# Layer 1's first shift and scale: from column-tiled matmuls in one attention stage to DVE row sums in the next

## The chip, the cores and the metric

The kernel runs on one core of a Trainium2 chip. The metric is the device time of one execution in microseconds (us). The core has five engines that work side by side, each through its own list of instructions in order: TensorE (PE, with its weight loads shown apart as PEld), VectorE (DVE), ScalarE (ACT), GpSimd (POOL) and SyncE (SP). Transfers between HBM and the core's memory (SBUF) are issued by SP or POOL and run on the DMA engines. TensorE writes to PSUM, eight banks of 512 fp32 values in each of 128 partitions.

## The reference, cut to what matters

The model has two layers over 512 latent tokens x and 256 context tokens ctx, all 1024 wide. Each layer turns the conditioning vectors (c for x, c_ctx for ctx) into six vectors of 1024 values: shift, scale and gate of the mixer, and the same three of the feed-forward part.

```
silu_c, silu_cc = silu(c), silu(c_ctx)
for layer in range(2):
    mod  = silu_c  @ w_mod[layer] + b_mod[layer]      # 6 x 1024 values, for x
    modc = silu_cc @ w_mod[layer] + b_mod[layer]      # 6 x 1024 values, for ctx
    sh1, sc1, g1, sh2, sc2, g2 = split(mod, 6)
    h  = rms_norm(x)   * (1 + sc1)  + sh1
    hc = rms_norm(ctx) * (1 + csc1) + csh1
    y, yc = mixer(h, hc)                              # layer 0: two kinds of attention
    x = x + g1 * y;   x = x + g2 * swiglu(norm(x, sc2, sh2))
    # the same two updates for ctx, in layer 0 only
```

The change concerns `sh1` and `sc1` of layer 1, for both streams: 2048 of the 6144 values of `mod` and of `modc`. These need the first 2048 columns of `w_mod[1]`, 8 MB in fp32, and are first used by the first norm of layer 1.

## The kernel before, in words

Work is feature-major: a stream is a tile of 128 partitions by 8 feature blocks by tokens. A projection multiplies in fp32 by splitting each operand in a high and a low part; `mm3` (L422 to L424) issues three matmuls for each block. `weight` (L133 to L145) loads a weight tile of 512 KB on SP's queue, rounds it on ACT (L143) and takes the rest on DVE (L145).

The program is written as Python generators. A main generator yields after each small step; `aside` keeps a list of other generators and `step(n)` advances them by n steps, so that their instructions are written between those of the main one. From this the framework's planner makes the order of each engine's list: of the instructions that are ready it takes those written first. A tile gets its memory when it is first used. A pool keeps, for each tag, a number of buffers (`bufs`); where all are in use, a new tile of this tag waits until the last access of the tile that holds one, wherever in the program this access is written. `keep_in_program_order` ties an instruction behind the one written just before it on the same engine; later ones may still pass it.

Layer 0 up to its output projection has these stages:

1. The input projection (`even_in`). The residual X (tile `xx`, 2 MB, the only buffer of its tag in pool `xz`) has been read by then. `rest()` takes that buffer anew as `xs` and `self.scratch`, and its quarters serve as `raws`, four buffers for modulation weights. `mods(0, 1)` and `mods(0, 2)` run aside (layer 0's other four vectors).
2. The first attention stage: attention of the 256 context tokens (8 head pairs), the rest of the queries, and the first 2 (`N1`) of the 8 head pairs of the latent tokens. PSUM: a=4, e=2, v=2 banks. Aside, at half a step for each step (`F0`): what is left of the queries, then `mods(1, 0)`, the subject of the change.
3. The second attention stage: the other 6 latent head pairs (`main`; 60 steps). PSUM: a=3, e=2, v=1, b=2. Aside, at 0.8 of a step for each (`F1`), `ctx_rest`: layer 0's output projection, norm and feed-forward part of the context stream, 76 weight tiles. It uses bank tag `b`, and `self.scratch` as room for squares and activations (`sq_a1`, `sq1`, `nm_t1`, `ff_a1`).
4. X is loaded again (`self.stream(0, self.ins["xt"])`, L200), and the latent stream's output projection (`onto`) follows, beside layer 1's context chain and `mod_rows(1, range(16, 48))`, which computes the other four vectors of layer 1, for x alone, as row sums on DVE.

In an attention step (`attend`, L628 to L652), PE writes the scores to `a` banks, DVE takes the maximum and adds the bias (L635, L639), ACT takes the exponential (L640, L642), PE transposes the result through two `e` banks (L650), DVE and ACT copy it out (L652), and PE multiplies it with the values (L678). At the end of a pair `normalise` uses a POOL copy (L664) and an `e` bank (L374).

`mods` holds the vector silu(c), padded to 32 columns, as the stationary operand in four column strips of the array at once and streams the weights past it (L230), 256 matmuls and 16 transfers of 512 KB on POOL's queue (L218) for one group of 2048 values; it holds one `e` bank while a quarter is accumulated, then copies (L240), transposes (L244) and adds the bias (L248). `mod_rows` spreads silu(c) along the free dimension once (transposes through `spread`, L374, and a copy, L264), and then has, for every 128 values, one transfer of 512 KB (L272) and one DVE instruction that multiplies and sums (L279).

Of the kernel before, what the change touches and what calls it, by code (L numbers as in the profile page):

```python
# [13 lines left out]
ALU = mybir.AluOpType  # L14
# [3 lines left out]
P = 128  # L18
NX, NCTX = 512, 256
NT = NX + NCTX  # L20
KD = 8
# [16 lines left out]
MI, F0, F1, O0 = 3, 0.5, 0.8, 1.4  # L38
M0, C1, B0, B1, B2, L0, L1, L2, L3 = 0.5, 1.6, 24, 2.3, 0.1, 0.5, 1.75, 1.4, 1.7

MG = 2

H0, H1, H2, H3 = 2, 2, 4, 4

# [25 lines left out]
class Net:  # L70
# [132 lines left out]
    def mods(self, l, g, tmp, raws, dma, tag="t", hold=False):  # L203
# [48 lines left out]
                yield  # L252
        yield

    def mod_rows(self, l, tiles, tmp, dma, tag):


        nc, V = self.nc, self.nc.vector
        s = self.t(tmp, [P, 1024], "silu_r", bufs=1)
        for h in range(2):  # L260
            ps = self.bank(tag)
            for j in range(4):
                self.spread(ps[:, P * j : P * j + P], self.sc[:, 4 * h + j, 0:1].broadcast_to([P, P]))
            nc.scalar.copy(s[:, 512 * h : 512 * h + 512], ps)  # L264
        V.memset(self.mod[l][:, tiles[0] : tiles[-1] + 1, 1], 0.0)
        todo, ahead = iter(tiles), []

        def load():
            t = next(todo, None)
            if t is not None:  # L270
                ahead.append(self.t(tmp, [P, 1024], "wmod", bufs=3))
                dma(ahead[-1], self.ins[f"wmodT{l}"][t - tiles[0]])  # L272

        load(), load(), load()
        yield
        for t in tiles:
            w = ahead.pop(0)
            self.tc.keep_in_program_order(
                V.tensor_tensor_reduce(w, w, s, 1.0, self.bmod[:, l, t : t + 1], ALU.mult, ALU.add, self.mod[l][:, t, 0:1])  # L279
            )  # L280
            load()
            yield
# [560 lines left out]
    def layer0(self):  # L843
        nc, V = self.nc, self.nc.vector
        with ExitStack() as c1:
# [8 lines left out]
            with ExitStack() as c2:  # L854
                ap_ = self.pool(c2, "attn0", 1)
                aq = ap_
                kst = self.t(ap_, [P, 8, NT], "kst", F32R)
                raws = [self.t(ap_, [P, 8, NX], f"qx{i}") for i in range(2)]
                vt = self.t(ap_, [P, TTILES, 256], "vt")
                cq = c2.enter_context(ExitStack())  # L860
                ap_ = self.pool(cq, "attnc", 1)
                tmp = Slots(self.t(ap_, [P, 16 * NCTX], "qc"), 2)
                start = self.start(tmp, [r[:, 4 * i : 4 * i + 4, :] for r in raws for i in range(2)], {0: hx, 1: hc})
                next(start)
                cp = self.cp
                self.cp = aq
                self.mband = self.const("mband", [P, 3 * P])
                self.sinkc = self.t(aq, [P, 8, 4], "sinkc")
                sk = self.const("sink", [P, 8])
                V.memset(self.sinkc, NEG)  # L870
                V.tensor_copy(self.sinkc[:, :, 0], sk)
                self.cp = cp
                c3 = c2.enter_context(ExitStack())
                tmp = self.pool(c3, "in0", 1)
                self.cp = tmp
                self.cos, self.sin = self.const("cos", [P, XTILES, HD]), self.const("sin", [P, XTILES, HD])
                self.cp = cp
                qx = qc = spare = None

                def rest():  # L880
                    nonlocal qx, qc, raws, spare
                    qx = [self.t(aq, [P, 8, NX], f"qx{i}", F32R) for i in range(2)]
                    qc = self.t(ap_, [P, 2, 8, NCTX], "qc", F32R)
                    qc = [qc[:, i] for i in range(2)]
                    xs = self.scratch = self.t(self.xz, [P, KD, NX], "xx")
                    cs = self.t(self.xz, [P, KD, NCTX], "xc").rearrange("p k n -> p (k n)")
                    raws = [xs[:, 2 * i : 2 * i + 2, :] for i in range(4)]
                    spare = Slots(cs, 2)
                    self.qg, self.kg = (self.t(spare, [P, HD], i, bufs=1) for i in ("qg", "kg"))
                    nc.gpsimd.dma_start(self.qg, self.ins["qg"])  # L890
                    nc.gpsimd.dma_start(self.kg, self.ins["kg"])
                    self.aside(*[self.mods(0, g, spare, raws, nc.gpsimd.dma_start) for g in (1, 2)[:MG]])
                    V.tensor_scalar(self.qg, self.qg, SCALE, None, op0=ALU.mult)
                    tabs = []
                    for g in (self.qg, self.kg):
                        C, S = self.t(tmp, [P, XTILES, HD], "gc", bufs=2), self.t(tmp, [P, XTILES, HD], "gs", bufs=2)
                        gb = g.unsqueeze(1)
                        V.tensor_tensor(C, self.cos, gb.broadcast_to([P, XTILES, HD]), op=ALU.mult)
                        for a, b in ((0, 32), (32, 0)):
                            V.tensor_tensor(  # L900
                                S[:, :, a : a + 32], self.sin[:, :, a : a + 32],
                                gb[:, :, b : b + 32].broadcast_to([P, XTILES, 32]), op=ALU.mult,
                            )
                        tabs.append((C, S))
                    (self.cq, self.sq), (self.ck, self.sk) = tabs
                    return list(zip(qx, qc))

                queries = self.even_in(tmp, hx, hc, kst, vt, start, rest)
                self.finish()
                cw.close()  # L910
                cps.close()
                with ExitStack() as cA:
                    tmp = self.pool(cA, "at0", 3, side="right")
                    xy = [(hx[0][y], hx[1][y]) for y in range(KD)]
                    cy = [(hc[0][y], hc[1][y]) for y in range(KD)]

                    def pairs(i, ys, blocks, q):
                        for br in range(2):
                            for pr in range(4):
                                yield self.even_pair(tmp, br, pr, blocks, q[br], kst, vt, ys[4 * br + pr])  # L920

                    def chain(gens):
                        for g in gens:
                            yield from g

                    main = chain(itertools.islice(pairs(0, xy, range(4), qx), N1, None))
                    with ExitStack() as c4:
                        self.psum(c4, a=4, e=2, v=2)
                        self.aside(queries, *[self.mods(*g, spare, raws, nc.gpsimd.dma_start, "e") for g in ((0, 1), (0, 2), (1, 0))[MG:]])
                        side = chain(itertools.islice(pairs(0, xy, range(4), qx), N1))  # L930
                        for i, _ in enumerate(chain(pairs(1, cy, (4, 5), qc))):
                            if i % 4 < N1:
                                next(side, None)
                            self.step(F0)
                        for _ in side:
                            self.step(F0)
                        self.finish()
                    c3.close()
                    cq.close()
                    with ExitStack() as c4:  # L940
                        self.psum(c4, a=3, e=2, v=1, b=2)
                        self.aside(self.ctx_rest(hc))
                        for _ in main:
                            self.step(F1)
                        self.finish()
            cC.close()
            self.stream(0, self.ins["xt"])
            self.layer1_open()
# [778 lines left out]
def prep(inputs):  # L1727
# [3 lines left out]
    g = {k: np.asarray(v) for k, v in inputs.items()}  # L1731
    f32 = np.float32
    c_ = np.ascontiguousarray
    d = {}
# [2 lines left out]
    cc = np.stack([g["c"][0], g["c_ctx"]], 1).reshape(KD, P, 2).transpose(1, 0, 2)  # L1737
    for l in range(2):
        for h in range(3):
            if (l, h) < (1, 1):  # L1740
                w = g["w_mod"][l][:, 2048 * h : 2048 * h + 2048].reshape(KD, P, 4, 4, P).transpose(3, 1, 0, 2, 4)
                d[f"wmod{l}{h}"] = c_(w.reshape(4, P, KD, 4 * P))
    d["wmodT1"] = c_(g["w_mod"][1][:, 2048:].T.reshape(32, P, KD * P))
    bmod = g["b_mod"].reshape(2, 48, P).transpose(2, 0, 1)
    nr = np.stack([g["norm_mix"][0], g["norm_ffn"][0], g["norm_mix"][1], g["norm_ffn"][1], g["norm_out"]])
    nr = nr.reshape(5, KD, P).transpose(2, 0, 1)
# [1 line left out]
    w = g["w_in_even"][0]  # L1748
# [3 lines left out]
    def tiles(w):  # L1752
        k, n = w.shape
        return w.reshape(k // P, P, n // P, P).transpose(2, 1, 0, 3).reshape(n // P, P, k)
# [17 lines left out]
    w = tiles(g["w_in_odd"][0])  # L1772
    d["w1in"] = c_(w)
    t = np.arange(P)
# [31 lines left out]
    i, j = np.arange(P)[:, None], np.arange(P)[None, :]  # L1806
# [21 lines left out]
```

## Time and profile before

| | us |
|---|---|
| median of 3 runs (2052.88 to 2057.1) | 2054.01 |
| the profiled execution | 2053.72 |
| its span, first to last instruction | 2051.9 |
| PE busy in the span | 1956.0 |
| DVE busy | 1261.4 |
| ACT busy | 893.7 |

The profile is of one execution. Busy time is the time in which an engine's records lie; matmul records overlap, since matmuls are pipelined, so the distance between starts tells what one costs in a row of them. A row of a group view gives line, engine, operation, tiles (out<-in), shapes and count, then the busy time in us and the mean of one in ns, then the idle time just before them and what ended it. A row of a timeline gives start, length (both us), engine, line, operation, tiles and count, and in brackets an idle time before it and its releaser. A row of the windows view gives start:end, length, then for each engine busy us and count, the granted clock of TensorE (1.00 is full), the mean share of the DMA engines and GB/s.

### The profile page before, as it was taken

How to read it: one execution, taken by the hardware profiler on the slowest of the kernel's cores; microseconds unless marked ns; L12 is line 12 of the kernel's file. 1: busy time of each engine (PE TensorE's matmuls, PEld its weight loads, DVE VectorE, ACT ScalarE, POOL GpSimd, SP SyncE). 2: the span in 40 equal slices, each digit the busy share in tenths (PEclk: the TensorE clock that was granted, in tenths of full speed). 3: DMA queues.
4: the chain of work that ended last, by engine and by line, in shares of the span. 5: the costliest groups of instructions: out<-in, count | busy, mean ns of one | idle time of the engine just before them, and what ended most of it. 6: DMA issues, size and time to landing. Idle time of an engine off the chain costs nothing.

```text
span 2051.9 us, 37913 instructions
## 1 busy us (share of the span) xinstructions
PE 1956.0 (95%) x15360; PEld 1606.6 (78%) x15360; DVE 1261.4 (61%) x2504; ACT 893.7 (44%) x1681; POOL 163.0 (8%) x326
## 2 busy tenths in 40 slices
PE   7999999999988999999999999899899989999997
PEld 6776778999987888777777777677667778888887
DVE  5656667666657554659746767787757773333335
ACT  4335556766733433553222346545345453222221
POOL 0111100000010001000112000102322000000000
PEclk9999999999999999999999999999799999999999
DMA  7453422434484345545533323455665133332321
GB/s 277 148 182 124 145 91 74 145 115 128 133 268 141 109 128 164 157 147 154 179 125 117 111 73 98 130 173 174 171 198 146 52 98 113 93 101 85 106 90 50
DMA packets 109918, 272.64 MB, mean 133 GB/s; under 512 B 14736, under 2 KB 48176, under 8 KB 106800
## 3 DMA queue, kind: packets, MB, share of 16 engines
q1 hardware_dynamic: 97520, 224.74, 35.5%
q0 software_dynamic: 12224, 45.49, 6.8%
q8 instruction: 121, 1.98, 0.4%
q14 instruction: 53, 0.43, 0.1%
HBM read 238.20 MB, written 31.98 MB: 132 GB/s over the span
## 4 chain that ended last, share of the span: by engine, by line
PE 78%; DVE 10%; issue 6%; DMA 3%; ACT 2%; POOL 0%; DVEq 0%; ACTq 0%; SPq 0%; POOLq 0%
PE ps_b L422 17%; PE ps_b L423 17%; PE ps_b L424 17%; PE ps_v L678 4%; PE ps_a L628 2%; PE ps_e L650 2%; PE ps_w L1351 2%; PE ps_w L1357 2%; DVE wlo L145 1%; PE ps_s L1380 1%; DMA xx<-in_wmod 1%; PE ps_w L1370 1%; PE ps_e L1258 1%; PE ps_w L1389 1%; DVE kb L1295 1%
## 5 line engine op out<-in xcount | busy, mean ns | idle before, releaser
L143 ACT CAST whi<-wraw 128x1024 fp32r<-128x1024 f32 (+2 forms) x291 | 292.6, 1008 | 664.1 <-PE ps_b L423 526.3
L145 DVE TENSOR_TENSOR wlo<-wraw,whi 128x1024 fp32r<-128x1024 f32 (+2 forms) x291 | 340.8, 1172 | 235.5 <-ACT whi L143 229.3
L422 PE MATMUL ps_b<-hxh,whi 128*128 128x512 f32 (+1 forms) x1040 | 402.4, 390 | 15.8 <-ACT cj L1018 6.7
L423 PE MATMUL ps_b<-hxl,whi 128*128 128x512 f32 (+1 forms) x1040 | 398.4, 385 | 2.1 <-DVE hxl L415 1.9
L424 PE MATMUL ps_b<-hxh,wlo 128*128 128x512 f32 (+1 forms) x1040 | 396.6, 383 | 2.2 <-DVE wlo L145 2.2
L422 PEld LDWEIGHTS ps_b<-hxh,whi 128*128 128x128 f32 x1040 | 199.1, 193 | 59.0 <-ACT cj L1018 7.2
L423 PEld LDWEIGHTS ps_b<-hxl,whi 128*128 128x128 f32 x1040 | 199.2, 192 | 40.7 <-DVE hxl L415 3.8
L424 PEld LDWEIGHTS ps_b<-hxh,wlo 128*128 128x128 f32 x1040 | 199.5, 193 | 39.7 <-DVE wlo L145 3.3
L422 PE MATMUL ps_b<-act,whi 128*128 128x512 f32 (+1 forms) x570 | 198.9, 349 | 6.5 <-ACT whi L143 3.3
L424 PE MATMUL ps_b<-act,wlo 128*128 128x512 f32 (+1 forms) x570 | 197.4, 346 | 2.1 <-DVE wlo L145 2.1
L423 PE MATMUL ps_b<-act,whi 128*128 128x512 f32 (+1 forms) x570 | 196.4, 345 | 0.4 <-DVE act L124 0.4
L422 PE MATMUL ps_b<-hch,whi 128*128 128x256 f32 x552 | 159.9, 290 | 4.2 <-ACT cj L982 2.1
L424 PE MATMUL ps_b<-hch,wlo 128*128 128x256 f32 x552 | 156.4, 284 | 0.8 <-DVE wlo L145 0.7
L423 PE MATMUL ps_b<-hcl,whi 128*128 128x256 f32 x552 | 156.0, 283 | 0.0
L422 PEld LDWEIGHTS ps_b<-act,whi 128*128 128x128 f32 x570 | 109.2, 192 | 21.7 <-issue 4.3
L424 PEld LDWEIGHTS ps_b<-act,wlo 128*128 128x128 f32 x570 | 109.1, 191 | 16.1 <-DVE wlo L145 3.3
L423 PEld LDWEIGHTS ps_b<-act,whi 128*128 128x128 f32 x570 | 109.1, 191 | 13.3 <-DVE act L124 0.8
L754 DVE TENSOR_TENSOR ff_a<-ff_a,ps_b 128x512 f32<-128x512 f32 x44 | 30.2, 687 | 134.3 <-PE ps_b L424 133.6
L422 PEld LDWEIGHTS ps_b<-hch,whi 128*128 128x128 f32 x552 | 104.9, 190 | 8.7 <-ACT cj L982 2.6
L424 PEld LDWEIGHTS ps_b<-hch,wlo 128*128 128x128 f32 x552 | 104.7, 190 | 1.9 <-DVE wlo L145 1.5
L455 DVE SCALAR_TENSOR_TENSOR xx<-ps_b,mod,xx 128x512 f32<-128x512 f32 (+1 forms) x64 | 43.7, 684 | 101.0 <-PE ps_b L424 100.6
L423 PEld LDWEIGHTS ps_b<-hcl,whi 128*128 128x128 f32 x552 | 105.1, 191 | 0.9 <-issue 0.2
(375 smaller groups left out, 3332.2 us busy)
## 6 DMA issues: line engine op xcount, KB each, us to landing
wraw<-in_ffi SPq DMA_DIRECT2D x132, 512.0 KB, 3.6
xx<-in_wmod POOLq DMA_DIRECT2D x48, 512.0 KB, 4.9
wraw<-in_w1in SPq DMA_DIRECT2D x43, 512.0 KB, 3.7
wraw<-in_ffo SPq DMA_DIRECT2D x48, 448.0 KB, 3.3
wmod<-in_wmodT POOLq DMA_DIRECT2D x32, 512.0 KB, 3.9
wraw<-in_ffo SPq DMA_DIRECT2D x24, 512.0 KB, 3.6
op<-op SPq DMA_DIRECT2D x32, 384.0 KB, 3.8
qx<-in_wmod SPq DMA_DIRECT2D x8, 1024.0 KB, 10.6
```

Of the source, the lines that this page charges most:

```text
L143: self.nc.scalar.copy(hi[:, 0:n], raw)
L145: e.tensor_tensor(lo[:, 0:n], raw, hi[:, 0:n].bitcast(F32), op=ALU.subtract)
L422: mm(out, lhsT=wh, rhs=hh, start=first, stop=False)
L423: mm(out, lhsT=wh, rhs=hl, start=False, stop=False)
L424: mm(out, lhsT=wl, rhs=hh, start=False, stop=last)
L455: self.nc.vector.scalar_tensor_tensor(X[:, m, c], ps[:, 0:n][:, c], gate[:, m, i : i + 1], X[:, m, c], op0=ALU.mult, op1=ALU.add)
L628: nc.tensor.matmul(o, lhsT=q, rhs=k[:, b : b + o.shape[1]], start=i == 0, stop=i == len(passes) - 1)
L650: nc.tensor.transpose(pt[:, P * (j - c) : P * (j - c) + P], p[:, P * j : P * j + P], self.ident)
L678: self.nc.tensor.matmul(ps[HD * u : HD * u + HD, col : col + P], lhsT=vs[u][j], rhs=pts[u][:, j, :], start=j == 0, stop=j == nk - 1, tile_ ...
L754: V.tensor_tensor(a, a, pg[1][:, 0:w], op=ALU.mult)
L1351: mm(wy[HD * u + HD - W_ + r : HD * u + HD, p, :], lhsT=G[top[u], p, r:W_], rhs=VU[top[u], p, u, :], start=p == 0, stop=False, skip_group_ ...
L1357: mm(o, lhsT=AR[:, p, :], rhs=Sd[:, p, u, :], start=False, stop=not lat, skip_group_check=True)
```

## The change

`mods(1, 0)` is taken out of the first attention stage. The second attention stage has in its place a new generator, `mod_rows2`, for the first 16 tiles of 128 values and for both streams. Its room is a new tile of tag `xx` in pool `xz`, cut in four quarters of 128 x 1024: the spread silu(c), the spread silu(c_ctx), one buffer for weights and one for the products. The spreading goes through bank tag `e`. The generator is advanced after the main generator's steps 0, 3, 6 and so on; each advance issues one transfer on POOL's queue, and the next one the two row sums on it, each tied behind the DVE instruction written before it. What is left after the last step follows then. The weights lie in HBM as `wmodT1`, which now has all 48 tiles.

```
+    def silu_row(self, i, s, tag):
         for h in range(2):
             ps = self.bank(tag)
             for j in range(4):
-                self.spread(ps[:, P * j : P * j + P], self.sc[:, 4 * h + j, 0:1].broadcast_to([P, P]))
-            nc.scalar.copy(s[:, 512 * h : 512 * h + 512], ps)
+                self.spread(ps[:, P * j : P * j + P], self.sc[:, 4 * h + j, i : i + 1].broadcast_to([P, P]))
+            self.nc.scalar.copy(s[:, 512 * h : 512 * h + 512], ps)
+
+    def mod_rows2(self, l, tiles, room, dma, tag):
+        V = self.nc.vector
+        *ss, w, x = room
+        for i in range(2):
+            self.silu_row(i, ss[i], tag)
+        for t in tiles:
+            dma(w, self.ins[f"wmodT{l}"][t])
+            yield
+            for i in range(2):
+                self.tc.keep_in_program_order(
+                    V.tensor_tensor_reduce(x, w, ss[i], 1.0, self.bmod[:, l, t : t + 1], ALU.mult, ALU.add, self.mod[l][:, t, i : i + 1])
+                )
...
-                dma(ahead[-1], self.ins[f"wmodT{l}"][t - tiles[0]])
+                dma(ahead[-1], self.ins[f"wmodT{l}"][t])
...
-                        self.aside(queries, *[self.mods(*g, spare, raws, nc.gpsimd.dma_start, "e") for g in ((0, 1), (0, 2), (1, 0))[MG:]])
+                        self.aside(queries)
...
                         self.psum(c4, a=3, e=2, v=1, b=2)
                         self.aside(self.ctx_rest(hc))
-                        for _ in main:
+                        xs = self.t(self.xz, [P, KD, NX], "xx").rearrange("p (r k) n -> p r (k n)", r=4)
+                        rows = self.mod_rows2(1, range(16), [xs[:, i] for i in range(4)], nc.gpsimd.dma_start, "e")
+                        for i, _ in enumerate(main):
                             self.step(F1)
+                            if i % 3 == 0:
+                                next(rows, None)
                         self.finish()
+                        for _ in rows:
+                            pass
...
-    d["wmodT1"] = c_(g["w_mod"][1][:, 2048:].T.reshape(32, P, KD * P))
+    d["wmodT1"] = c_(g["w_mod"][1].T.reshape(48, P, KD * P))
```

More of the change, by code (lines that the diff above doesn't have):

```diff
@@ L39 @@
 M0, C1, B0, B1, B2, L0, L1, L2, L3 = 0.5, 1.6, 24, 2.3, 0.1, 0.5, 1.75, 1.4, 1.7
-MG = 2
 H0, H1, H2, H3 = 2, 2, 4, 4
@@ L253, in mods @@
         yield
+    def silu_row(self, i, s, tag):
+        for h in range(2):
+            ps = self.bank(tag)
+            for j in range(4):
+                self.spread(ps[:, P * j : P * j + P], self.sc[:, 4 * h + j, i : i + 1].broadcast_to([P, P]))
[12 more added lines that the diff above has]
+                )
     def mod_rows(self, l, tiles, tmp, dma, tag):
@@ L259, in mod_rows @@
         s = self.t(tmp, [P, 1024], "silu_r", bufs=1)
-        for h in range(2):
-            ps = self.bank(tag)
-            for j in range(4):
-                self.spread(ps[:, P * j : P * j + P], self.sc[:, 4 * h + j, 0:1].broadcast_to([P, P]))
-            nc.scalar.copy(s[:, 512 * h : 512 * h + 512], ps)
+        self.silu_row(0, s, tag)
         V.memset(self.mod[l][:, tiles[0] : tiles[-1] + 1, 1], 0.0)
@@ L891, in rest @@
                     nc.gpsimd.dma_start(self.kg, self.ins["kg"])
-                    self.aside(*[self.mods(0, g, spare, raws, nc.gpsimd.dma_start) for g in (1, 2)[:MG]])
+                    self.aside(*[self.mods(0, g, spare, raws, nc.gpsimd.dma_start) for g in (1, 2)])
                     V.tensor_scalar(self.qg, self.qg, SCALE, None, op0=ALU.mult)
@@ L1739, in prep @@
         for h in range(3):
-            if (l, h) < (1, 1):
+            if l == 0:
                 w = g["w_mod"][l][:, 2048 * h : 2048 * h + 2048].reshape(KD, P, 4, 4, P).transpose(3, 1, 0, 2, 4)
                 d[f"wmod{l}{h}"] = c_(w.reshape(4, P, KD, 4 * P))
-    d["wmodT1"] = c_(g["w_mod"][1][:, 2048:].T.reshape(32, P, KD * P))
+    d["wmodT1"] = c_(g["w_mod"][1].T.reshape(48, P, KD * P))
     bmod = g["b_mod"].reshape(2, 48, P).transpose(2, 0, 1)
```

## The prediction

> **What bounds the kernel now.** I read the page first, then the windows view over the stages that the change touches.
>
> ```profile
> span 2051.9 us, 37913 instructions
> ...
> PE 78%; DVE 10%; issue 6%; DMA 3%; ACT 2%; POOL 0%; DVEq 0%; ACTq 0%; SPq 0%; POOLq 0%
> ```
>
> ```profile
> 175.00:278.00 103.00, 96.87 (x944) 71.72 (x943) 73.44 (x214) 61.15 (x182) 12.04 (x23) 1.00 0.29 102
> 278.00:345.00 67.00, 65.32 (x543) 57.79 (x543) 48.70 (x116) 38.43 (x97) 0.61 (x1) 0.95 0.25 75
> 345.00:575.00 230.00, 229.42 (x2000) 219.94 (x2000) 150.19 (x300) 162.89 (x312) 6.76 (x9) 1.00 0.43 133
> 575.00:607.00 32.00, 25.20 (x184) 24.39 (x183) 21.35 (x46) 12.23 (x19) 2.22 (x6) 0.89 0.80 274
> ```
>
> The chain of waits lies on TensorE for 78% of the span. The columns of the windows are PE, weight loads, DVE, ACT, POOL. The first window is the first attention stage, from which the matmuls go; the other three are the second, into which the sums go. PE is the limit in both: 96.87 of 103, and 229.42 of 230 where attention and the context's projections are mixed. DVE has 80 of 230 us free there. So work taken off PE in the first stage pays, and DVE work in the second could cost nothing. Whether it does hangs on when it can run.
>
> **Removed: the matmuls.** The groups of 200 to 250 us, then PE's timeline:
>
> ```profile
> L230 PE MATMUL ps_e<-xx,silu_c 128*32 128x128 f32 x256 | 8.4, 275 | 0.7 <-DMA xx<-in_wmod 0.4 <-DVE sm_y L671 0.3
> ```
>
> ```profile
> 225.99 0.65 PE L230 MATMUL ps_e<-xx,silu_c 128*32 128x128 f32 x16 [0.38 <-DMA xx<-in_wmod]
> ...
> 243.89 1.95 PE L230 MATMUL ps_e<-xx,silu_c 128*32 128x128 f32 x64
> ...
> 287.10 0.82 PE L650 MATMUL ps_e<-ident,sm_p 128*128 128x128 f32 x6
> ```
>
> All 256 lie here: 64 in 1.95 us, so 7.8 us, and 0.7 us of waits. The 16 transposes cost about 0.11 us each, by six of the same shape in 0.82 us with 0.27 us for the last to end: 1.8 us. An e bank comes free too. I take 10 us off the first stage, with bounds of 6 (part of it fills gaps that stay) and 14 (the bank pays as well). The 16 transfers of 512 KB are only moved; the DMA share here is 0.29, so no gain is counted for them.
>
> **Where the sums can start.** This step decides. Their room is a new tile of tag xx, which has one buffer. Its holder is `self.scratch`, which `ctx_rest` writes until its last square. The timelines of ACT, DVE, PE and SP's queue where this buffer is next handed on:
>
> ```profile
> 605.57 0.42 ACT L344 ACTIVATE xx<-xc 128x256 f32<-128x256 f32 x1 [1.32 <-DVE xc L455]
> ...
> 606.06 0.41 DVE L346 TENSOR_TENSOR xx<-xx 128x256 f32<-128x256 f32 x1
> ...
> 606.53 0.61 PE L354 MATMUL ps_b<-ones,xx 128*128 128x1 f32 x4 [1.86 <-DVE xx L346]
> ...
> 607.16 0.33 SPq L200 DMA_DIRECT2D xx<-in_xt x1
> ```
>
> The load of X, the buffer's next tenant, issues at 607.16, right behind the matmuls that read the last sums of squares. In the changed kernel the next tenant is the sums' room, written earlier in the program; it gets the buffer no earlier. The tie only keeps a sum from passing what was written before it; it cannot bring it ahead of the buffer.
>
> A second wait follows. `silu_row` is written after the first attention step and before that step's transposes. Its own transposes are ready at once and take both e banks; the ACT copies that would empty them write into the new room and wait. Attention needs e banks for every transpose, so it stops after the three softmax tiles that its pool holds. `ctx_rest` uses only b banks and needs nothing from this attention. I therefore expect the second stage to fall apart: the context's projections alone, then attention together with the sums.
>
> **The stage after the change.** It runs now from 278.78 to 607.38, 328.6 us. Its bounds, and the context's share, from PE's timeline, the groups of 278 to 607 us, and a window with nothing but these matmuls:
>
> ```profile
> 277.61 0.59 PE L374 MATMUL ps_e<-ident,sm_t 128*128 128x128 f32 x2 [0.80 <-POOL sm_t L664]
> 278.78 1.65 PE L628 MATMUL ps_a<-kst,qx 128*128 128x256 f32 x4 [0.58 <-DVE sm_y L671]
> ...
> 326.17 0.61 PE L354 MATMUL ps_b<-ones,xx 128*128 128x1 f32 x4
> ...
> 336.12 0.37 PE L422 MATMUL ps_b<-hch,whi 128*128 128x256 f32 x1
> ...
> 587.85 0.39 PE L422 MATMUL ps_b<-act,whi 128*128 128x256 f32 x1 [3.30 <-ACT whi L143]
> ...
> 607.38 0.50 PE L422 MATMUL ps_b<-hxh,whi 128*128 128x512 f32 x1 [0.25 <-DVE rms1x L106]
> ```
>
> ```profile
> L422 PE MATMUL ps_b<-hch,whi 128*128 128x256 f32 x416 | 120.9, 291 | 0.0
> ...
> L422 PE MATMUL ps_b<-act,whi 128*128 128x256 f32 x176 | 52.3, 297 | 3.3 <-ACT whi L143 3.3
> ```
>
> ```profile
> 596.00:604.00 8.00, 8.00 (x69) 1.00 0.61 217
> ```
>
> *Context alone.* Three matmuls for each of 416 + 176 is 1776; at 8.00/69 = 0.116 us that is 206 us, and 211 with a few us for records that the window may lack. The norm between (326.17 to 336.12) is filled by attention now and would be bare: 10 us, and 2 for its slow start. I add 5 for late weights such as the 3.30. Sum 228; bounds 218 (half of the stalls) and 245 (the clock of 0.89 for half of it).
>
> *Attention and sums.* DVE's groups of 278 to 578 us, then the row sum as the kernel already does it, then its transfer:
>
> ```profile
> L652 DVE COPY sm_t<-ps_e 128x384 f32<-128x384 f32 x48 | 26.4, 550 | 2.5 <-PE ps_e L650 2.4
> L635 DVE TENSOR_REDUCE sm_m<-ps_a 128x1 f32<-128x260 f32 x32 | 13.7, 427 | 0.9
> L639 DVE CUSTOM_DVE_ANT_0 sm_p<-ps_a,zero,sm_m 128x512 f32<-128x512 f32 x16 | 12.0, 749 | 3.9 <-PE ps_a L628 3.5
> ...
> L639 DVE CUSTOM_DVE_ANT_0 sm_p<-ps_a,c_mband,sm_m 128x384 f32<-128x384 f32 x16 | 9.9, 617 | 2.1
> ...
> L639 DVE CUSTOM_DVE_ANT_0 sm_p<-ps_a,c_mband,sm_m 128x256 f32<-128x256 f32 x16 | 7.7, 482 | 1.7
> L635 DVE TENSOR_REDUCE sm_m<-ps_a 128x1 f32<-128x256 f32 x16 | 6.7, 420 | 4.4 <-PE ps_a L628 4.4
> L631 DVE COPY ps_a<-sinkc 128x4 f32<-128x4 f32 x32 | 5.1, 160 | 18.6 <-PE ps_a L628 18.5
> L671 DVE TENSOR_TENSOR sm_y<-sm_y,ps_e 128x512 f32<-128x512 f32 x6 | 4.1, 684 | 0.0
> L639 DVE DVE_READ_ACCUMULATOR2_ANT sm_m<- 128x1 f32 x48 | 4.0, 83 | 0.0
> ...
> L124 DVE TENSOR_TENSOR hxl<-sm_y,hxh 128x512 fp32r<-128x512 f32 x5 | 3.4, 688 | 0.7 <-ACT hxh L119 0.6
> ```
>
> ```profile
> L279 DVE CUSTOM_DVE_ANT_0 wmod<-wmod,silu_r,c_tab x32: 1274/1279/1740, 703.2 to 1133.8; 128x1024 f32<-128x1024 f32 x32
> L279 DVE DVE_READ_ACCUMULATOR2_ANT mod<- x32: 77/82/85, 704.4 to 1135.0; 128x1 f32 x32
> ```
>
> ```profile
> wmod<-in_wmodT POOLq DMA_DIRECT2D x32, 512.0 KB, 3.9
> ```
>
> The ten rows sum to 93.0 us; a missing sixth split and a dozen small sums and reciprocals make it some 96. The 32 row sums, 1.279 + 0.082 us each, add 43.5. DVE sets this part: 140 us of records. Its records overlap a little and it will have pauses; I let the two cancel and take 141. The lower bound is the chain of the sums with one weight buffer: 3.9 us for a transfer, 2 x 1.36 for the sums on it and some 0.3 of handover, 6.9 x 16 = 111 us. The upper bound is DVE busy 80% of the time, 176. Behind a sum that waits for its transfer stand attention's maxima and copies on DVE; on POOL's queue, behind a transfer that waits for the sums, stand the copies of `normalise`. The load of X on SP now waits for the last sum, but that one is written at step 48 of 60, so X arrives before attention ends.
>
> *Handover.* SP's queue shows when the next stage's weights are first asked for, and the page what their conversion costs:
>
> ```profile
> 575.98 0.33 SPq L133 DMA_DIRECT2D wraw<-in_w0out x1
> ```
>
> ```profile
> L143 ACT CAST whi<-wraw 128x1024 fp32r<-128x1024 f32 (+2 forms) x291 | 292.6, 1008 | 664.1 <-PE ps_b L423 526.3
> L145 DVE TENSOR_TENSOR wlo<-wraw,whi 128x1024 fp32r<-128x1024 f32 (+2 forms) x291 | 340.8, 1172 | 235.5 <-ACT whi L143 229.3
> ```
>
> That is where attention gives up its memory now, and the context's last 30 us hide the transfer and the conversion. With attention last they are bare: 3.9 us, as for the other transfers of 512 KB, and 1.01 + 1.17: 7 with the waits between; bounds 2 and 14, as other constants are loaded at the same moment.
>
> Sum: 228 + 141 + 7 = 376 against 328.6 is +47.4; less 10 is +37.4. On the profiled execution's 2053.7 (1.8 more than its span, 0.3 under the median of the runs) this makes **2091 us**. ACT's copies of silu(c) and 16 transposes of 0.11 us count as nothing here: both engines wait for DVE in that part; in a PE-bound stretch the transposes would cost 1.8.
>
> **The rivals.**
>
> *The sums do run under the projections* (not slower). If the room were to be had early, the 43.5 us would fit into DVE's 80 free us and only the 1.8 us of transposes would cost: 2053.7 - 10 + 1.8 = 2046. For it: the free DVE time. Against it: the handover at 607.16 and the one buffer. It decides if the first row sum starts before the context's last square.
>
> *Attention is not held up, the sums alone are late.* If attention kept its e banks, both would be mixed as now, and the sums would start at about 597, 10 earlier than 607. Then 111 us and some 5 for the spreading pass before X may load, at about 713 instead of 607.16, and the first update of X waits for it: +106, 2160. Against it: the place of `silu_row` ahead of the transposes.
>
> *PE's clock falls while it waits for DVE.* PE's records outside the 211 us of context are at most 65 + 229 + 25 - 211 = 108 us, so at full clock DVE stays the limit; at half clock PE would need up to 216 for the second part, 75 more than 141: up to 2166, and half of that if half of it is slow, 2129. Against it: the granted clock is 1.00 in the first attention stage, where PE is fed in the same small pieces. For it: 0.89 in the window with pauses (575 to 607).
> The Trainium skill ("TensorE: Matmul & The Clock Gate", section on the HAM clock gate) says that the array's clock is halved after an idle window of some 3.4 us and comes back after as long a busy one; by it short pauses cost nothing, and the clock of 1.00 agrees.
>
> **How the numbers follow.** The forecast has 0.80, the early sums 0.07, the late sums 0.06, the slow clock 0.07. The forecast's own bounds, all taken at one end, are 218 + 111 + 2 - 328.6 - 14 = -12, and 245 + 176 + 14 - 328.6 - 6 = +100; that all fall to one side is unlikely, and 60% of the way from +37.4 gives 2062 to 2129 as its own range. The range that I give, 2056 to 2135, is a little wider for half a slow clock, and leaves out the early and the late sums. This kernel's runs tell 0.2%, 4 us, from no change: slower by more is 0.90 (nearly all of the forecast, and the two slow rivals), faster 0.07, within it 0.03.
>
> **What would show it.** Right: `ctx_rest`'s matmuls in one stretch of about 230 us from 270 with hardly any transposes between; the first row sum only after its last square, near 500; a stretch of some 140 us with DVE nearly full and PE about half used; the output projection near 645. Wrong: row sums between 280 and 500; or PE full from 345 to 575 as now; or DVE well under 80% in the last stretch, by which the 141 would be too small.

## The result, and the profile after

The changed kernel takes 2108.43 us (median of 4 runs, 2105.02 to 2113.33) against 2053.45 us for the kernel before beside it (2052.56 to 2057.1). The ratio is 1.0271, with a 95% interval of 1.0253 to 1.0289: slower by 55.7 us (52 to 59). The forecast was 2091 in a range of 2056 to 2135. The profiled execution took 2106.97 us.

The page first: the chain of waits still lies on TensorE (it was 78%), with DVE's share up from 10%.

```profile
span 2105.2 us, 37556 instructions
...
PE 76%; DVE 11%; issue 6%; DMA 3%; ACT 3%; POOL 1%; SPq 0%; DVEq 0%; ACTq 0%; POOLq 0%
```

PE's timeline of the changed kernel (start, length, line, tiles, count, and in brackets how long PE was idle and on what) shows the stage fall in two:

```profile
268.69 1.09 PE L645 MATMUL ps_a<-kst,qx 128*128 128x256 f32 x5 [0.58 <-DVE sm_y L688]
...
269.62 0.27 PE L391 MATMUL ps_e<-ident,silu_c 128*128 128x128 f32 x1
...
269.84 0.93 PE L391 MATMUL ps_e<-ident,silu_c 128*128 128x128 f32 x7
...
271.28 0.28 PE L439 MATMUL ps_b<-hch,whi 128*128 128x256 f32 x1
...
499.11 0.28 PE L441 MATMUL ps_b<-act,wlo 128*128 128x256 f32 x1
500.93 0.61 PE L371 MATMUL ps_b<-ones,xx 128*128 128x1 f32 x4 [1.54 <-DVE xx L363]
502.22 1.97 PE L391 MATMUL ps_e<-ident,silu_c 128*128 128x128 f32 x8 [0.68 <-ACT xx L260]
504.01 0.90 PE L667 MATMUL ps_e<-ident,sm_p 128*128 128x128 f32 x3
```

ACT's timeline shows the copies that empty the two e banks:

```profile
501.58 1.07 ACT L260 COPY xx<-ps_e 128x512 f32<-128x512 f32 x2 [1.16 <-PE ps_b L371]
```

The second stage begins at 268.69 instead of 278.78. Half of the 16 transposes of silu(c) run at once (1 and 7) and fill both e banks. They are copied out only at 501.58, released by the matmuls of the context's last sum of squares (L371); the other half follow at 502.22 and attention's own transposes (L667) at 504.01. Between lie the context's projections. The row sums, by their line (shortest, median and longest in ns, then the first and the last start):

```profile
L273 DVE CUSTOM_DVE_ANT_0 xx<-xx,c_tab x32: 1274/1276/1286, 506.8 to 624.3; 128x1024 f32<-128x1024 f32 x32
```

And the windows of the two halves, and of the start of the output projection (up to the context's first normalisation, `nm_t`), after and then before:

```profile
268.69:502.00 233.31, 224.84 (x1812) 221.25 (x1812) 138.67 (x205) 103.56 (x157) 0.29 (x3) 0.98 0.50 159
502.00:647.50 145.50, 123.40 (x930) 92.40 (x930) 118.77 (x312) 77.50 (x245) 15.02 (x25) 0.92 0.23 75
650.53:706.31 55.78, 50.70 (x246) 42.18 (x246) 31.39 (x65) 13.75 (x18) 1.60 (x4) 0.89 0.66 226
```

```profile
607.38:654.44 47.06, 47.05 (x250) 40.80 (x250) 27.35 (x59) 12.69 (x17) 0.82 (x4) 0.96 0.58 187
```

In the first half PE is all but full and DVE is idle for 95 us; in the second neither is full: PE 123.4 and DVE 118.8 of 145.5, with a clock of 0.92. The output projection starts at 650.53 instead of 607.38 (+43.2) and loses 8.7 more in its start, where PE was full before and is now idle for 5 us. That makes +51.9 where `nm_t` begins; the spans differ by 53.3. Nearly the whole loss stands before 710 us. The longest pause of PE in that start:

```profile
663.47 0.80 PE L439 MATMUL ps_b<-hxh,whi 128*128 128x512 f32 x1 [4.64 <-ACT whi L142]
```

### The profile page after: what moved, and what is told of

Read it like the earlier page. It is cut to its first block, busy times and chain, and to the rows that moved or that the text cites. A ratio compares the mean times of both kernels' runs of the same rounds, so it can differ in the third digit from the quotient of the medians.

```text
span 2105.2 us, 37556 instructions
## 1 busy us (share of the span) xinstructions
PE 1979.8 (94%) x15116; PEld 1614.2 (77%) x15116; DVE 1303.0 (62%) x2564; ACT 863.8 (41%) x1653; POOL 161.7 (8%) x326
## 4 chain that ended last, share of the span: by engine, by line
PE 76%; DVE 11%; issue 6%; DMA 3%; ACT 3%; POOL 1%; SPq 0%; DVEq 0%; ACTq 0%; POOLq 0%
PE ps_b L439 17%; PE ps_b L440 17%; PE ps_b L441 17%; PE ps_v L695 3%; PE ps_a L645 2%; PE ps_w L1374 2%; PE ps_e L667 2%; PE ps_w L1380 2%; PE ps_s L1403 1%; PE ps_w L1393 1%; PE ps_e L1281 1%; DVE wlo L144 1%; PE ps_w L1412 1%; DVE kb L1318 1%; DVE xx L273 1%
## 6 DMA issues: line engine op xcount, KB each, us to landing
qx<-in_wmod SPq DMA_DIRECT2D x8, 1024.0 KB, 10.1
```

## The experiments

The theory: the one buffer of tag xx, and through `silu_row` the two e banks, hold attention back until the context is done. The rivals: the 43.5 us of sums cost wherever they stand; the loss is in the handover. Line numbers shift by a few between the kernels. Differences in us are ratios times 2053.5.

**The removal alone.** Layer 1's first shift and scale are set to zero and not computed.

```diff
-                        xs = self.t(self.xz, [P, KD, NX], "xx").rearrange(...)
-                        rows = self.mod_rows2(1, range(16), ...)
...
-                            if i % 3 == 0:
-                                next(rows, None)
+                        V.memset(self.mod[1][:, 0:16, :], 0.0)
```

> The changed kernel without the row sums, their room and their rows of silu(c): layer 1's first shift and scale are set to zero instead of being computed. If the held buffer is what costs, this leaves only the gain of the removed matmuls, 10 us: 2043 (2039 to 2048), and the second stage is mixed as in the kernel before (TensorE full from 345 to 575 less 10). If something else in the changed kernel costs (the new order of the weights, say), it stays above 2053.

Measured: 2043.89 us, ratio 0.9944 (0.992 to 0.9967): -11.5 us. The second stage's window:

```profile
268.83:595.57 326.74, 317.82 (x2722) 300.10 (x2722) 219.96 (x461) 213.43 (x428) 9.99 (x17) 0.99 0.45 136
```

It begins 9.95 us earlier than before and is 326.7 long against 328.6. The versions that take the matmuls away and do the sums elsewhere are compared with this.

**The hold without the sums.** The room, the rows of silu(c) and the transfers stay; the shift and the scale are not computed.

```diff
             dma(w, self.ins[f"wmodT{l}"][t])
             yield
-            for i in range(2):
-                self.tc.keep_in_program_order(V.tensor_tensor_reduce(x, w, ss[i], ...))
+            if t == 15:
+                V.tensor_tensor(self.mod[l][:, 0:16, :], w[:, 0:32]..., ss[0][:, 0:32]..., op=ALU.mult)
```

> The changed kernel with its room, its rows of silu(c) and its 16 transfers, but without the 32 row sums (one small product stands in their place, so layer 1's first shift and scale are not computed). Held buffer: the context's projections still run alone from 270 to about 502; then attention alone, on TensorE some 108 us and on DVE some 97 instead of 144, so about -35 against the changed kernel: 2073 (2064 to 2085), still slower than before. If the row sums' own time on DVE is the cost, and the hold costs nothing: at or below 2054.

Measured: 2088.11 us, ratio 1.0155 (1.0122 to 1.0188): +31.8, above the expected 2064 to 2085, but far from 2054. Its windows, context and then attention:

```profile
273.50:506.00 232.50, 224.49 (x1811) 220.97 (x1811) 138.34 (x202) 103.12 (x156) 0.13 (x2) 0.98 0.54 159
506.00:624.00 118.00, 110.14 (x930) 84.44 (x929) 81.47 (x249) 76.11 (x244) 12.35 (x23) 0.99 0.29 90
```

The context alone takes as long as with the sums. Attention alone takes 118 us; PE is busy for 110 of it and DVE for 81. So the hold costs 31.8 + 11.5 = 43 us against the removal alone, with not one sum in it, and the sums add 55.7 - 31.8 = 24. With them PE's records in that half grow from 110 to 123 at a clock of 0.92 instead of 0.99, and its idle time from 8 to 22 us. The 16 transfers on POOL's queue wait for the same buffer; no run has the rows of silu(c) in it without these transfers, so what each of the two would hold up alone is not shown.

**All sums after attention.**

```diff
                         for i, _ in enumerate(main):
                             self.step(F1)
-                            if i % 3 == 0:
-                                next(rows, None)
```

> The changed kernel with the same room, but the rows of silu(c) and all sums written after attention's last step. Held buffer: attention keeps its banks and is mixed with the projections as before, until about 597; then the chain of transfer and two sums for 16 tiles, 111 us, before X can be loaded: 2160 by the prediction's price of late sums (2130 to 2170; the lower end if the chain takes 5.5 us a tile with little else on the queues). If the hold is not what counts but the sums' time on DVE: as the changed kernel, 2108, or less.

Measured: 2159.43 us, ratio 1.0503 (1.0476 to 1.053). The stage in a window, the sums by their line, and SP's queue:

```profile
270.16:595.20 325.04, 316.74 (x2727) 299.05 (x2727) 219.66 (x459) 213.41 (x428) 9.29 (x16) 0.99 0.44 136
```

```profile
L273 DVE CUSTOM_DVE_ANT_0 xx<-xx,c_tab x32: 1279/1285/1286, 601.5 to 708.5; 128x1024 f32<-128x1024 f32 x32
...
  DMA xx<-in_wmodT: 61.3, 16
```

```profile
709.91 0.33 SPq L199 DMA_DIRECT2D xx<-in_xt  x1
```

With `silu_row` behind attention's transposes, attention and projections are mixed again: 325 us, PE full. The sums then stand alone at 7.0 us for each weight (107 us from the first sum's start to the last's: 15 periods and one sum), and X's load waits for the last. This is the prediction's second rival, priced at 2160 with X loaded at 713.

**Room of its own.** `ctx_rest` uses 1792 of the scratch tile's 4096 columns. One row of silu(c) and one weight fit beside it; the streams come one after the other, so each weight is loaded twice.

```diff
-        *ss, w, x = room
+        s, w = room
         for i in range(2):
-            self.silu_row(i, ss[i], tag)
-        for t in tiles:
-            dma(w, ...); yield
-            for i in range(2): ... (x, w, ss[i], ...)
+            self.silu_row(i, s, tag)
+            for t in tiles:
+                dma(w, ...); yield; ... (w, w, s, ...)
...
-                        xs = self.t(self.xz, [P, KD, NX], "xx").rearrange("p (r k) n -> p r (k n)", r=4)
+                        xs = self.scratch.rearrange("p (r k) n -> p r (k n)", r=4)      # rows 2 and 3
...
-                            if i % 3 == 0:
+                            if i % 5 < 3:
```

> The sums get room that is free in time: one row of silu(c) and one weight in the half of the scratch tile that the context's projections don't use; both streams after one another, so 32 transfers instead of 16, one sum for each. Held buffer: the sums run between the steps of attention while the projections go on, and the stage is as long as before but for 1.8 us of transposes: 2046 (2042 to 2052). If the 43.5 us of sums on DVE cost wherever they stand: 2053.5 - 10 + 43.5 = 2087 or near it, and no less than 2065.

Measured: 2057.15 us, ratio 1.0009 (0.9994 to 1.0024). The window of the stage and the group of the sums:

```profile
268.68:608.99 340.31, 328.23 (x2739) 306.31 (x2739) 255.07 (x526) 214.33 (x430) 24.49 (x48) 0.97 0.57 178
```

```profile
L272 DVE CUSTOM_DVE_ANT_0 xx<-xx,c_tab 128x1024 f32<-128x1024 f32 x32 | 41.0, 1280 | 6.0 <-DMA xx<-in_wmodT 5.9
```

The same number of sums in the same stage, in another buffer: 54 us faster than the changed kernel. That shows the buffer to be the cause, and the rival of sums that cost their full 43.5 us falls. But the expected 2046 was missed too: against the removal alone the stage is 13.6 us longer, though DVE is busy for only 255 of 340 us.

**Where these 13 us lie.** Five kernels. The first loads only one of the 32 weights, so that it computes other values:

```diff
-                dma(w, self.ins[f"wmodT{l}"][t])
+                if t == 0 and i == 0:
+                    dma(w, self.ins[f"wmodT{l}"][t])
```

> The kernel with the sums in their own room, where only the first of the 32 weights is loaded and all sums work on it (scaled by 0.25, so layer 1's first shift and scale are wrong values). It asks where the 13 us went that the own room costs over the removal alone (2057 against 2044). If the sums wait on DVE for their transfers (6.0 us in the own room's groups) and hold up what is queued behind them, most of that comes back: 2047 to 2051. If it is the DVE time of the sums between the steps, it stays near 2057 (2054 to 2058).

Measured: 2052.42 us, ratio 0.9988 (0.9972 to 1.0003); the stage is 334.0 us long. In these two traces about half of the 13.6 goes with the transfers; 7.3 stay with sums that wait for nothing. By the ratios it is 4 us of 13, and the intervals overlap.

The second does stream 1's 16 sums here and stream 0's with the later rows (`mod_rows` over 48 tiles, and the gain of that norm taken again when they are done); the third does stream 1's in the first attention stage, with three weight buffers in the then free scratch tile.

```diff
-M0, ... = 0.5, ...
+M0, ... = 0.75, ...
...
-                    rest = self.mod_rows(1, range(16, 48), wm, nc.gpsimd.dma_start, "m")
+                    rest = self.mod_rows(1, range(48), wm, nc.gpsimd.dma_start, "m")
...
+                self.norm_gain(1, 0, slice(0, None))
                 self.norm_lead(tmp, 1, 0, self.hx, ...)
```

> Stream 1's 16 sums, with the room in the scratch tile and one weight buffer, at every third step of the second attention stage; stream 0's 16 sums, needed only at layer 1's norm near 1150, with the 32 sums of the gate that run from 756 to 1185 (DVE is busy about half of that time there). If the price is per sum in this stage (13.3 us for 32): half of it, 2044 + 6.6 = 2051 (2046 to 2055). If the late sums cost as much in their stage: 2057.

> As the split before, but stream 1's 16 sums run in the first attention stage, where the scratch tile is free, with three weight buffers. DVE is busy 72 of 103 us there, and the sums take 22. If a sum between the steps costs only what it delays and its transfer is early: 2044 to 2050, the fastest of these. If the first stage has no more slack for DVE than the second: 2051, as the other split or above.

Measured: 2057.26 (ratio 1.0007, 0.9995 to 1.0019) and 2061.63 (1.0037, 1.002 to 1.0053). Neither gains. In the traces, against the removal alone, 16 sums lengthen the second stage by 6.4 us, the first by 11.5, and the stage from the output projection to layer 1's first norm by 5.3 (and 7.7): 0.3 to 0.7 us for a sum of 1.36, in each of three stages where DVE had time to spare. Each of these figures is from one execution.

The fourth puts a sum at every second step instead of three in five.

```diff
-                            if i % 5 < 3:
+                            if i % 2 == 0 or i > 54:
```

> The sums on DVE in their own room, one at every second step instead of three in five, so that each transfer of 3.9 us has a whole step more. If the waits on the transfers were what separated the own room (2057) from the one without transfers (2052): 2052 to 2054, no difference from the kernel before. If the price is per sum and transfer traffic: 2057.

Measured: 2050.71 us, ratio 0.9989 (0.9978 to 1.0001).

```profile
269.90:600.66 330.76, 318.93 (x2738) 300.89 (x2739) 256.91 (x526) 216.03 (x432) 24.43 (x48) 0.99 0.56 183
```

```profile
L272 DVE CUSTOM_DVE_ANT_0 xx<-xx,c_tab 128x1024 f32<-128x1024 f32 x32 | 40.9, 1279 | 9.1 <-DMA xx<-in_wmodT 9.1
```

The time came as expected, but not by the reason given: the waits for transfers rose from 6.0 to 9.1 us while the stage fell by 9.5.

A good part of these differences is TensorE's clock, which falls to half for short stretches. One stands in the own room's stage and not here:

```profile
316.68:324.68 8.00, 8.00 (x44) 5.64 (x44) 5.86 (x18) 3.49 (x10) 0.00 (x0) 0.57 0.26 72
```

Full clock less granted clock, summed over windows of 2 us, makes 8.5 us in the own room's stage, 5.1 without the loads, and 3.4 here and in the removal alone. So some 5 of the 13.6 us, and some 5 of the 9.5, are slow clock and not work on DVE. The profiled executions differ too: the own room's is one of its slowest (2062.00 of 2052.24 to 2062.48), this one's one of its fastest (2047.89 of 2047.37 to 2055.44). By the ratios the two kernels are 4 us apart, with intervals that overlap, so it is not shown that the place of the sums among attention's steps counts.

A last kernel took the waits away:

```diff
+                for h in range(2):        # a weight in two halves, a buffer for each; one half at every step
+                    ... (w, w, s[:, 512 * h : 512 * h + 512], 1.0, bmod or the first half's sum, ...)
```

> As the own room with a sum at every second step, but each sum in two halves of 512 columns, with a weight buffer for each half in the same room, one half at every step: a half's transfer has a whole step more to come. If the 9.1 us in which DVE stood before its sums for their transfers are what is left of the price (2051 against 2044 for the removal alone): 2046 to 2049, faster than before. If a sum's fixed cost counts (some 0.3 us for each instruction pair, 64 instead of 32: 10 us more of DVE): 2051 to 2055, no better than whole sums.

Measured: 2052.91 us, ratio 0.999 (0.9977 to 1.0002): no better. The waits fell to 3.5 us, and the 64 halves took 47.8 us of DVE instead of 40.9. Which instruction behind a sum passes its delay on to TensorE was not settled.

**The sums on GpSimd.** POOL is busy for only 10 of this stage's 327 us in the removal alone. It makes the products of half weights and folds them by adds to 16 columns; DVE adds these up once for each stream.

```diff
-                V.tensor_tensor_reduce(w, w, s, ...)
+                    nc.gpsimd.tensor_tensor(w, w, s[:, 512 * h : 512 * h + 512], op=ALU.mult)
+                    nc.gpsimd.tensor_tensor(...)      # halves added: 256, 128, 64, 32, 16 columns
...
+            V.tensor_reduce(self.mod[l][:, 0:16, i], col, AX.X, ALU.add)
```

> The sums leave DVE: in the free part of the scratch tile, each weight is loaded in two halves, and GpSimd makes the products (two of 512 columns) and folds them by adds down to 16 columns; DVE adds these up once for each stream. By this kernel's own rows (a product of 512 columns 1.05 us on POOL, 256 columns 0.71) a sum is some 5.5 us of POOL, 175 us for 32 of the stage's 327. If what the own room cost over the removal is DVE's time and the waits on it: 2044 + 2 of transposes and slack = 2046 to 2050, faster than both kernels. If POOL's work slows DVE, or attention's copies on POOL wait behind the sums: 2057 or more.

Measured: 2138.37 us, ratio 1.041 (1.0391 to 1.0429), far above even the 2057 or more that was expected if POOL slowed the others. The waits between 395 and 450 us, and the groups on POOL and on DVE:

```profile
DVE mod L297 <- POOL mcol L294: 31.4, 1, 31.4
ACT act L118 <- DVE xx L795: 30.5, 1, 30.5
PEld ps_b L465 <- DVE wlo L144: 29.4, 1, 29.4
PE ps_b L465 <- DVE wlo L144: 29.2, 1, 29.2
```

```profile
L286 POOL TENSOR_TENSOR xx<-xx 128x512 f32<-128x512 f32 x62 | 85.8, 1383 | 6.7 <-ACT xx L260 6.0
...
L144 DVE TENSOR_TENSOR wlo<-wraw,whi 128x1024 fp32r<-128x1024 f32 x49 | 75.5, 1542 | 19.5 <-ACT whi L142 19.2
```

The kernel before has four POOL products of 512 columns, in a later stage, and the same split on DVE in this one:

```profile
L1400 POOL TENSOR_TENSOR Vx<-Vx,bon x4: 1042/1042/1061, 1518.1 to 1583.2; 128x512 f32<-128x512 f32 x4
...
L145 DVE TENSOR_TENSOR wlo<-wraw,whi 128x1024 fp32r<-128x1024 f32 x60 | 73.3, 1222 | 33.4 <-ACT whi L143 33.2
```

DVE's one addition for stream 0 stood in DVE's queue for 31.4 us until POOL's last fold was there, and everything behind it stood too; that of stream 1 did so for 21.4. And both engines' instructions are longer side by side: the product of 512 columns takes 1.38 us instead of 1.04 in the kernel before, DVE's split of a weight 1.54 instead of 1.22. DVE's copies of 384 columns out of PSUM took 0.55 us in both kernels. The Trainium skill ("GPSIMD Engine Reference", section 8, Key points) says that GpSimd shares its SBUF interfaces with VectorE and contends with VectorE instructions of two SBUF inputs; DVE's split has two and its copy has none, and the rows agree.

The next kernel moves the two additions behind the stage's last step in the program:

```diff
                 yield
-            V.tensor_reduce(o, col, AX.X, ALU.add)      # for each stream, in the loop
+        for i in range(2):
+            V.tensor_reduce(o, col[:, i], AX.X, ALU.add)
```

> The sums on GpSimd again, but DVE's two final additions, which stood in DVE's queue for 31 us until POOL's last sum was there, come behind the stage's last step. If those two waits made the loss: 2138 less 2 x 31 = 2076 or less, and PE full from 400 to 450. What is left over 2046 is then the price of POOL and DVE working side by side: in the kernel before it DVE's split of a weight took 1.52 us instead of 1.20, 0.32 x 76 = 24 us of DVE, and 0.3 of each on the path would be some 7: 2053 to 2076. If POOL's copies for attention stuck behind the sums were the cause, it stays above 2100.

Measured: 2117.29 us, ratio 1.0314 (1.0291 to 1.0338). Its waits between 270 and 680 us:

```profile
DVE mod L299 <- POOL mcol L295: 36.7, 2, 34.3
```

Of the two waits one is down to 2.4 us, the other still lasts 34.3: the additions were not tied to the program's order, and the first of them still stood in DVE's queue ahead of work that it held up. So 20 us came back, about the second wait's 21.4, and the price of the shared work alone stays unmeasured.

**The handover.** The changed kernel, with one line more:

```diff
                 self.early(self.ins["w0out"][0])
+                self.fetch(self.ins["w0out"][1])
```

> The changed kernel with the second weight of the output projection asked for right behind the first, ahead of the constants and the bias table on SP's queue. If the late second weight (4.64 us of TensorE's wait at 663 and the slow clock behind it) is what the forecast's handover left out: 5 to 10 us faster than the changed kernel, 2098 to 2103. If the transfers share the DMA engines so that order changes nothing: 2108.

SP's queue in the changed kernel, then here:

```profile
645.46 0.33 SPq L132 DMA_DIRECT2D wraw<-in_w0out  x1
...
648.25 0.33 SPq L95 DMA_DIRECT2D c_mu<-in_mu  x1
...
652.85 0.65 SPq L1074 DMA_DIRECT2D ob_r<-in_rpb  x1
654.81 0.33 SPq L132 DMA_DIRECT2D wraw<-in_w0out  x1
```

```profile
652.17 0.80 SPq L132 DMA_DIRECT2D wraw<-in_w0out  x2
654.96 0.33 SPq L95 DMA_DIRECT2D c_mu<-in_mu  x1
```

The window of the projection's start here:

```profile
657.19:707.70 50.51, 48.87 (x246) 40.96 (x246) 30.86 (x65) 13.77 (x18) 1.66 (x4) 0.94 0.74 247
```

Measured: 2104.17 us, ratio 1.0241 (1.0213 to 1.027), 6 us under the changed kernel by the ratios, though the intervals overlap. In the trace the stretch from the first matmul of the output projection to `nm_t` falls from 55.8 to 50.5 us (47.1 before): some 5 of the 8.7 us are the late second weight. The trace does not show where all 6 us of the whole come from: its attention part is 6.7 us longer than in the changed kernel's trace, and `nm_t` begins 1.4 us later there.

## Why the prediction was right

The time and the hold came as forecast; the loss, 55.7 us, is half as large again as the forecast 37.4.

*The removal*: 10 us (6 to 14) in the first stage. Measured 10.1 at the second stage's start, and 11.5 in all.

*Where the sums can start*: the deciding step held in both its parts. The first sum came at 506.8, after the last square; half of the transposes filled the e banks at 269.8; the second rival's kernel, which leaves the room and undoes only the hold of attention, gives that rival's time to 1 us; and the kernel with other room loses the hold altogether.

*The context alone*: 228 (218 to 245), measured 233.3. The size nearly held, its terms less so. The matmuls came every 0.120 us, 213 us in all against 211. No matmul of this part waited for a weight, for which 5 us stood in the sum; the slow clock behind the norm cost 5 us (24 us from 292 to 316 at 0.79) instead of 2; and attention's opening and the last sum of squares lie in the stretch too.

*Attention and sums*: 141 (111 to 176), measured 145.5. The size held, its working did not. "DVE sets this part: 140 us of records" is the step that failed. DVE was busy for 82%, not nearly all. Attention without sums takes 118 us, not the 96 counted for DVE's records (DVE is busy for 81 of it), and it is PE, busy for 110 of it, that comes nearest to setting it; the sums then add 27.5, not 43.5. The two errors cancel, which is luck.

*The handover*: 7 (2 to 14), measured 3.0 from 647.5 to 650.53 (5.1 from the weight's request at 645.46). But it was ended at the first matmul, and this is the term that was too small: behind it the second weight's request stood in SP's queue after seven constants and the bias table, PE waited, and 8.7 us went. The term was named in its upper bound ("other constants are loaded at the same moment"), but only for the first weight.

With these the sum is 233.3 + 145.5 + 3.0 - 328.6 - 10.1 = +43.1, and 8.7 behind it make 51.9 of the spans' 53.3; the forecast's +37.4 was low by 5 in the context, 4.5 in attention and 9 in the start of the projection, less 4 in the handover.

*The rivals.* Early sums were priced at 2046; done by other room they gave 2057 and 2051. The reason, that they fit into DVE's 80 free us, doesn't hold in full: they fit, and the stage was still 4 and 14 us longer than in the removal alone, 5 of the 14 by the clock. That instructions behind a sum pass its delay on to PE is likely, but no run shows which do. Late sums (2160) gave 2159. The slow clock was half there: 0.92 in the second half, 13 us more of PE's records, part of the 27.5 and not beside it.

## What to carry to other kernels

Before work is put into an engine's idle time, follow its buffers: a tile whose tag has one buffer can be written only after the last use of the tile that holds it, and whatever is issued meanwhile on its behalf (here 8 transposes into two PSUM banks) stays in the way of all others who need those resources. Idle time on an engine that works in order is not free: in single traces, the clock's part included, sums of 1.36 us cost 0.1 to 0.7 us each in stages where DVE had a fifth or more of its time to spare, so 10 us of matmuls are not worth trading for 43 us of such work. With the hold gone, the best versions (2050.71 and 2052.91, ratios 0.9989 and 0.9990 with intervals that reach 1) are level with the kernel before, and none beat it.

## What the runs showed of the hardware that was not expected

TensorE's clock can fall behind pauses of 1.4 to 2.3 us. PE's timeline, and windows, of the changed kernel:

```profile
558.94 0.44 PE L667 MATMUL ps_e<-ident,sm_p 128*128 128x128 f32 x2 [1.39 <-DVE sm_t L669]
...
581.02 1.97 PE L695 MATMUL ps_v<-sm_t,vt 128*64 128x128 f32 x14 [2.25 <-DVE sm_t L669]
```

```profile
557.00:559.00 2.00, 0.61 (x4) 0.37 (x5) 2.00 (x5) 0.00 (x0) 0.29 (x1) 1.00 0.00 0
559.00:561.00 2.00, 2.00 (x19) 1.50 (x20) 1.85 (x7) 0.73 (x2) 0.24 (x1) 0.73 0.41 102
561.00:563.00 2.00, 1.71 (x6) 1.23 (x6) 1.05 (x4) 1.39 (x7) 0.00 (x0) 0.50 0.41 160
```

The granted clock goes from 1.00 to 0.50 within 2 us behind a pause of 1.39 us, and the longest pause that the timeline shows in the whole second half is 2.25. The rule of the Trainium skill that the prediction named (an idle window of some 3.4 us), read as one unbroken pause, would have left the clock alone here; the measurement decides. The same attention without sums, with 8 us of pauses instead of 22 in all, kept 0.99. Full clock less granted clock, summed over windows of 2 us, makes 11.9 us in the second half against 1.7 without sums: 10 of the 27.5 us that the sums add.

The length of a pause alone does not decide it. The last sum of squares follows a pause of 1.86 us in the kernel before (at 606.53) and in the kernel with room of its own:

```profile
608.13 0.61 PE L370 MATMUL ps_b<-ones,xx 128*128 128x1 f32 x4 [1.86 <-DVE xx L362]
```

The 5 us from there on, in the kernel before and in the other:

```profile
606.53:611.53 5.00, 4.75 (x17) 3.77 (x18) 3.77 (x15) 0.00 (x0) 1.67 (x6) 0.73 1.01 330
```

```profile
608.13:613.13 5.00, 4.75 (x22) 3.97 (x23) 3.78 (x15) 0.00 (x0) 1.68 (x6) 1.00 0.97 324
```

The same work behind the same pause lost the clock in one execution and kept it in the other. What else decides is not shown.

The other surprise is the size of what POOL and DVE take longer side by side, a third on POOL's products and a quarter on DVE's splits, in the rows above.
